# The 18 emptiest experts two by two in one block, with float32 products on two halves of the columns

## The chip, the core and the metric

The kernel runs on one core of a Trainium2 chip. The metric is device time in microseconds (us) of one launch. Of the engines, PE (TensorE) multiplies matrices, DVE (VectorE) and ACT (ScalarE) work elementwise, POOL (GpSimd) issues the indexed transfers here, and SP (SyncE) issues the others. The profile is of one execution.

## The reference

A decoder block: two token mixers side by side (HGRN2 and gated DeltaNet), merged and added to the input, then a mixture of experts, then a final norm. There are 1024 tokens of width 1024 behind 16 learned meta tokens that are dropped at the end. Cut to the part that the change touches:

```python
grp = argmax(g_logits)                         # 4 groups of 8 experts
top_p, top_i = top_k(softmax(e_logits[grp]), 2)
weights = p_grp * top_p / sum(top_p)           # two experts per token
for each expert e, over its tokens x:
    y = (silu(x @ w_gate[e]) * (x @ w_up[e])) @ w_down[e]   # 1024 -> 512 -> 1024
    out[token] += weight * y
return rmsnorm(h + out)
```

There are 32 experts, each with 6 MiB of float32 weights. How many tokens an expert has is known on the chip alone. With the inputs of these runs the fullest of the first 29 experts has 137 tokens, the next ten 65 or more, and the other 18 have 36 to 63; experts 29, 30 and 31 have 60, 53 and 56.

## The kernel before

The mixers fill the first 1000 us or so. What follows is a loop over experts, one step each, in the order 31, 30, 29, 0 to 28. A table made on the chip (`tabi`, `rowi`, `wsl`) says for each expert which rows of the normed stream fill its block of `CB = 112` rows, where the result goes, and with what weight. `pick` finds the fullest of experts 0 to 28 and trades its place with expert 12 (`PQ`); that step works on two blocks (a column `NE` of the table holds the second). Any further rows over 112 would go to a loop at the end that runs only if there are some (`overflow` makes its table; here it has none).

A step works like this. Six transfers of 1 MiB each (`fetch`, issued by SP: gate 2, up 2, down 2) bring the weights into a ring of 12 buffers (`raws`); towards the end the ring shrinks to four, one buffer every 16 transfers from the sixtieth on, because the buffers are wanted for the output. `wload` splits each half of such a buffer in a high and a low part in float32r: ACT copies the high part (line 60) and DVE subtracts it from the source (line 61). When both halves are split, the buffer is free for the next transfer. Rows of tokens are gathered by POOL (line 1233), transposed (line 1244) and split in the same way. `stage_gu` makes three products for each piece, high by high, low by high and high by low (lines 1261 to 1263): 48 products of 512 columns for gate and up. `stage_h` transposes the activation (line 1279) and `stage2` makes 24 more products for down (lines 1299 to 1301). ACT scales the result, and POOL adds it to the residual stream in DRAM by an indexed transfer with accumulation, the scatter (line 1310): 112 rows of 4 KB, whether a row holds a token or a spare row.

The down products of a step stand behind the gate and up products of the next one in TensorE's program, since they wait for the activation (`pend`). The last expert is not scattered; its result is added to the output tiles by products with a one-hot matrix (line 1417), and the final norm follows (from line 1378 on).

Of the kernel before, what the change touches and what calls it, by code (L numbers as in the profile page):

```python
# [19 lines left out]
P = 128  # L20
# [12 lines left out]
def block_kernel(ctx, tc, x, meta_tokens, hg_lb_logits, norm_mix_g, w_in, gd_conv_w, gd_A_log, gd_dt_bias,  # L33
# [191 lines left out]
    NE, NX, CB = 32, 20, 112  # L225
    PQ = 12
    ND = NE - 3
    NT = SEQ // CB
    NB = NE + NX
# [9 lines left out]
    ionb = iota("ionb", NB)  # L239
# [815 lines left out]
    S0, S1 = slice(0, ND), slice(NE, NB)  # L1055
    tabbed = rows(ptb[:, ND:NE], slice(ND, NE))
    tab1 = r_("tab1", [P, NE])
    V.tensor_copy(tab1, ptb[:, 0:NE])
    pei = r_("pei", [1, NE], I32)
    ohx = r_("ohx", [P, NE])  # L1060
    nohx = r_("nohx", [P, NE])
    pxx = r_("pxx", [P, NE])
    ptx = r_("ptx", [P, 1])

    def pick(after):

        with tc.issue_after(after.ins):
            cnt = off[:, NC:NC + 1, 0:ND]
            V.memset(ohx, 0.0)
            first_max("px", cnt, ND, ohx[:, None, 0:ND])  # L1070
            V.tensor_scalar(nohx, ohx, -1.0, 1.0, op0=ALU.mult, op1=ALU.add)
            V.tensor_copy(pxx, ionb[:, 0:NE])
            trade(pxx)
            V.tensor_copy(pei, pxx[0:1])
            trade(tab1)
            return rows(tab1[:, S0], S0)

    def trade(t):
        m = r_next([P, NE])
        V.tensor_tensor(m, t, ohx, op=ALU.mult)  # L1080
        V.tensor_reduce(out=ptx, in_=m, op=ALU.add, axis=AX.X)
        V.tensor_tensor(m, t, nohx, op=ALU.mult)
        V.scalar_tensor_tensor(t, ohx, t[:, PQ:PQ + 1], m, op0=ALU.mult, op1=ALU.add)
        V.tensor_copy(t[:, PQ:PQ + 1], ptx)

    def r_next(shape):
        return rp.tile(shape, F32, name="ptm", tag="ptm")
# [3 lines left out]
    def weigh(after):  # L1091

        with tc.issue_after(after.ins):
# [13 lines left out]
            V.tensor_copy(wsl[:, 0:NE], pw[:, 0:NE])  # L1107
            V.tensor_tensor(wsl[:, 0:NE], wsl[:, 0:NE], pw[:, NE:], op=ALU.add)
            trade(wsl[:, 0:NE])
# [4 lines left out]
    def overflow():  # L1114

        gtx = r_("gtx", [P, NE, NT])
# [3 lines left out]
        zne = r_("zne", [P, NE])  # L1120
# [46 lines left out]
        V.scalar_tensor_tensor(xe, xo, pxx[0:1, PQ:PQ + 1], xe, op0=ALU.mult, op1=ALU.add)  # L1167
# [9 lines left out]
    XB, RMIN, DROP = 2, 4, 16  # L1177
# [8 lines left out]
    for pool, tag, n, b in ((mix, "xl", 4, 1), (rawp, "tg", 1, 1), (rawp, "oh", 2, 1), (wp, "wr", 0, 2), (tl, "bo", 2, 2),  # L1186
                            (mix, "xh0", 2, 1)):
        if n == 0:
            raws.append([pool.tile([P, 1024], F32, name=f"rawh{i}", tag=tag, bufs=b) for i in range(2)])
        else:  # L1190
            t_ = pool.tile([P, n, 2048], F32, name="raw" + tag, tag=tag, bufs=b)
            raws += [[t_[:, i, 0:1024], t_[:, i, 1024:], t_[:, i]] for i in range(n)]
# [5 lines left out]
    sg, hh0 = (wp.tile([P, 512], F32, name="msg" + str(i), tag="st", bufs=3) for i in range(2))  # L1198
    hT = mo.tile([P, 2, 4, CB], F32R, name="hT")
    turn = {"h": 0, "l": 0, "x": 0, "y": 0}  # L1200
# [7 lines left out]
    def fetch(load, src, q):  # L1208
        if nraw[0] > 60 and nraw[0] % DROP == 0 and len(ring) > RMIN:
            ring.pop(0)  # L1210
        wr = raws[ring[0]]
        ring.append(ring.pop(0))
        nraw[0] += 1
        if len(wr) == 2:
            for a in range(2):
                load(wr[a], src, q * 2048 + a * 1024, 1024)
        else:
            load(wr[2], src, q * 2048, 2048)
        return wr

    def wload(load, src, q):
        wr = early.pop(0) if early else fetch(load, src, q)
        nuse[0] += 1
# [8 lines left out]
    def gather(xg, gidx):  # L1232
        nc.gpsimd.indirect_dma_start(out=xg[:CB], out_offset=None, in_=hf_dr,
                                     in_offset=bass.IndirectOffsetOnAxis(ap=gidx[:CB], axis=0),
                                     bounds_check=SEQ, oob_is_err=False)
# [37 lines left out]
    def stage_h(hhs):  # L1273
        r = []
        for i, hh in enumerate(hhs):
# [4 lines left out]
            if i:  # L1280
                hx = rp.tile([P, 2, 4, CB], F32R, name="hx", tag="ohs1")
                hTh, hTl = hx[:, 0], hx[:, 1]
            else:
                hTh, hTl = hT[:, 0], hT[:, 1]
# [24 lines left out]
    def scatter(yt, ridx):  # L1309
        nc.gpsimd.indirect_dma_start(out=h2_dr, out_offset=bass.IndirectOffsetOnAxis(ap=ridx[:CB], axis=0),  # L1310
                                     in_=yt[:CB], in_offset=None, bounds_check=SEQ + P, oob_is_err=False,
                                     compute_op=ALU.add)
# [14 lines left out]

    order = list(range(NE - 1, ND - 1, -1)) + list(range(ND))
    gq = [(n, e) for n, o in enumerate(order) for e in ([PQ, NE] if o == PQ else [o])]
    got = []  # L1330

    def ahead(m):

        while len(got) < len(gq) and gq[len(got)][0] <= m:
            i, e = len(got), gq[len(got)][1]
# [4 lines left out]
            gather(xg, tabi[:, e:e + 1])  # L1340
            got.append(xg)

    def gathered(n):
        ahead(n)
        return [stage_x(got[i]) for i in range(len(gq)) if gq[i][0] == n]


    for e, srcs in ((0, (wg_e, wu_e)), (1, (wg_e, wu_e)), (0, (wd_e,)), (2, (wg_e, wu_e))):
        early += [(by_expert(order[e]), src, q) for src in srcs for q in range(2)]
    early = [fetch(*a) for a in early[:len(raws)]]  # L1350

# [3 lines left out]
    for n, e in enumerate(order):  # L1355
        load = by_expert(e) if e >= ND else by_index(pei[:, e:e + 1])
        if n == NE - 1:
            stage2(*pend)
# [114 lines left out]
```

## Time and profile before

| | us |
|---|---|
| median of 3 runs | 1655.86 (1651.85 to 1659.97) |
| the profiled execution | 1652.94 |
| its span in the trace | 1651.1 |
| PE busy | 1574.7 (95%) |
| DVE busy | 1081.5 |
| ACT busy | 796.1 |
| POOL busy | 224.1 |

The granted clock of TensorE was 0.981 of its full 2.4 GHz in the mean. The span runs from the first to the last instruction of the core; the profiled execution's own time is 1.8 us longer. The share of time in which an engine is busy says nothing yet of which one sets the pace, because the mixers and the expert loop have different limits. The loop is therefore read by windows of time, and from the waits inside these.

### The profile page before, as it was taken

The numbers are of one execution on the slowest core, as the hardware profiler recorded it, in microseconds if no ns is written. First come the engines' busy times: TensorE is split into PE (matmuls) and PEld (weight loads), VectorE is DVE, ScalarE is ACT, GpSimd is POOL, SyncE is SP. The second block draws the span as 40 slices with busy tenths as digits, with TensorE's granted clock in tenths as the row PEclk, the third lists the DMA queues.
The fourth block names the chain that finished last, engine by engine and source line by source line (L and its number), as shares of the span: only waits on it lengthen the run. The fifth ranks groups of instructions, "written<-read, shape, count | busy, mean of one in ns | idle before, by whom it ended". The sixth has DMA issues, their size and how long they took to land. (4 is left out here: it accounts for less than half of the span.)

```text
span 1651.1 us, 27239 instructions
## 1 busy us (share of the span) xinstructions
PE 1574.7 (95%) x10434; PEld 1301.8 (79%) x10434; DVE 1081.5 (66%) x1774; ACT 796.1 (48%) x1171; POOL 224.1 (14%) x172
## 2 busy tenths in 40 slices
PE   6999999999999999999999986999999999999984
PEld 6989898788788778788797885777777777777762
DVE  7224566368367364232647547999999689998976
ACT  6122222332331432322333233888888678888873
POOL 2150000010010010000001012651111111111112
PEclk9999999999999999999999997999999999999996
DMA  6264344344335235267847665999999999999994
GB/s 207 69 208 137 103 129 121 97 128 138 114 103 159 72 89 139 59 181 251 248 140 231 204 230 175 358 332 375 380 371 385 308 316 375 363 363 363 364 343 191
DMA packets 197894, 368.20 MB, mean 223 GB/s; under 512 B 29980, under 2 KB 136670, under 8 KB 175360
## 3 DMA queue, kind: packets, MB, share of 16 engines
q1 hardware_dynamic: 174464, 320.14, 55.9%
q0 software_dynamic: 8320, 23.08, 6.2%
q10 hardware_dynamic: 14976, 23.21, 4.0%
q8 instruction: 83, 1.36, 0.3%
q14 instruction: 51, 0.42, 0.1%
HBM read 311.05 MB, written 62.07 MB: 226 GB/s over the span
## 5 line engine op out<-in xcount | busy, mean ns | idle before, releaser
L284 PE MATMUL pj<-xh,wh 128*128 128x512 f32 (+2 forms) x832 | 307.6, 370 | 0.0
L286 PE MATMUL pj<-xh,wl 128*128 128x512 f32 (+2 forms) x832 | 306.8, 369 | 0.0
L285 PE MATMUL pj<-xl,wh 128*128 128x512 f32 (+2 forms) x832 | 305.9, 368 | 0.0
L284 PEld LDWEIGHTS pj<-xh,wh 128*128 128x128 f32 x832 | 156.7, 188 | 17.1 <-issue 0.2
L286 PEld LDWEIGHTS pj<-xh,wl 128*128 128x128 f32 x832 | 156.8, 188 | 16.7 <-issue 0.6
L285 PEld LDWEIGHTS pj<-xl,wh 128*128 128x128 f32 x832 | 156.6, 188 | 15.9
L345 ACT ACTIVATE st<-pj 128x512 f32<-128x512 f32 (+2 forms) x104 | 54.8, 527 | 169.7 <-PE pj L286 161.8
L1263 PE MATMUL pgu<-mwl,xTs 128*112 128x512 f32 x318 | 126.0, 396 | 0.0
L61 DVE TENSOR_TENSOR wl<-wr,wh 128x1024 fp32r<-128x1024 f32 x44 | 53.7, 1220 | 83.2 <-ACT wh L60 73.1
L1261 PE MATMUL pgu<-sx,xTs 128*112 128x512 f32 x264 | 107.0, 405 | 0.0
L60 ACT ACTIVATE mwh<-rawxl 128x1024 fp32r<-128x1024 f32 x86 | 90.5, 1059 | 33.3 <-PE pgu L1262 22.0
L1262 PE MATMUL pgu<-sx,xTs 128*112 128x512 f32 x264 | 104.8, 397 | 0.8 <-DVE xTs L61 0.8
L1261 PE MATMUL pgu<-mwh,xTs 128*112 128x512 f32 x264 | 104.2, 395 | 0.0
L1262 PE MATMUL pgu<-mwh,xTs 128*112 128x512 f32 x264 | 103.7, 393 | 0.0
L60 ACT ACTIVATE sx<-rawxl 128x1024 fp32r<-128x1024 f32 x84 | 87.9, 1059 | 30.9 <-PE pgu L1262 14.6
L60 ACT ACTIVATE wh<-wr 128x1024 fp32r<-128x1024 f32 x44 | 46.6, 1058 | 108.1 <-PE pj L285 87.6
L309 POOL TENSOR_TENSOR rn<-ss,mhalf 128x4 f32<-128x4 f32 x16 | 20.6, 1286 | 535.9 <-DVE ss L320 305.7
L1310 POOL DMA_INDIRECT h_dr<-h,rowi x32 | 61.8, 1932 | 218.5 <-ACT h L1305 203.9
L1263 PE MATMUL pgu<-sx,xTs 128*112 128x512 f32 x210 | 83.6, 398 | 0.1
L61 DVE TENSOR_TENSOR mwl<-rawxl,mwh 128x1024 fp32r<-128x1024 f32 x57 | 69.3, 1223 | 13.1 <-ACT mwh L60 10.8
L1023 PE MATMUL pyo<-wo,mm 128*128 128x256 f32 x256 | 73.6, 288 | 3.7 <-ACT mm L1001 3.7
L1024 PE MATMUL pyo<-wo,mm 128*128 128x256 f32 x256 | 72.7, 284 | 0.0
(615 smaller groups left out, 3760.4 us busy)
## 6 DMA issues: line engine op xcount, KB each, us to landing
rawxl<-in_w_up_dram SPq DMA_DIRECT2D x36, 1024.0 KB
rawxl<-in_w_down_dram SPq DMA_DIRECT2D x33, 1024.0 KB
wr<-in_w_in_dram SPq DMA_DIRECT2D x44, 512.0 KB
rawbo<-in_w_down_dram SPq DMA_DIRECT2D x19, 1024.0 KB
rawxl<-in_w_gate_dram SPq DMA_DIRECT2D x16, 1024.0 KB
rawxh<-in_w_gate_dram SPq DMA_DIRECT2D x15, 1024.0 KB
rawbo<-in_w_gate_dram SPq DMA_DIRECT2D x13, 1024.0 KB
rawoh<-in_w_gate_dram SPq DMA_DIRECT2D x10, 1024.0 KB
```

The costliest lines, as they stand in the source:

```text
L60: act(out=hi, in_=src, func=AF.Copy)
L61: return eng.tensor_tensor(out=lo, in0=src, in1=hi.bitcast(F32), op=ALU.subtract)
L284: nc.tensor.matmul(ps[:, :n], wh[:, k], a, start=(k == 0), stop=False)
L285: nc.tensor.matmul(ps[:, :n], wh[:, k], b, start=False, stop=False)
L286: last = nc.tensor.matmul(ps[:, :n], wl[:, k], a, start=False, stop=(k == KD - 1))
L345: act(out=st[:, :n], in_=ps, func=func, scale=scale)
L1023: nc.tensor.matmul(ps[:, 0:256], mm[0][:, k, ts], wo[:, 0, k], start=(k == 0), stop=False)
L1024: nc.tensor.matmul(ps[:, 0:256], mm[0][:, k, ts], wo[:, 1, k], start=False, stop=False)
L1261: nc.tensor.matmul(ps[:CB], xTh[:, kk], wh[:, s], start=(kk == 0), stop=False)
L1262: nc.tensor.matmul(ps[:CB], xTl[:, kk], wh[:, s], start=False, stop=False)
L1263: nc.tensor.matmul(ps[:CB], xTh[:, kk], wl[:, s], start=False, stop=(kk == 7))
L1310: nc.gpsimd.indirect_dma_start(out=h2_dr, out_offset=bass.IndirectOffsetOnAxis(ap=ridx[:CB], axis=0), in_=yt[:CB], in_offset=None, bounds_ ...
```

## The change

The experts 0 to 28 are ranked by their count on the chip. `pick` makes one key per expert (count times 32, plus a number that breaks ties), counts for each how many keys are greater, makes a permutation matrix of these ranks, and by one product the list `pei` of experts in order of rank (line 1085). `ranked` permutes the columns of the row table by a transpose and four products (lines 1099 to 1107). Ranks 0 to 10 are worked on alone, as before, with the split weights and 112 rows (`stage_gu`, `stage2`; rank 0 has the second block, column `NBB`). Ranks 11 to 28 form nine pairs: rank 11 + p with rank 20 + p share one block of 128 rows, 64 (`CL`) each.

A pair's weights are not split. Its products take the float32 weights from the ring buffers as they come (`raw`), the token tile is not split either (`pair_x`), and the products of the two experts stand alternately on the first and the last 64 columns of the array (`pair_mm`): 16 and 16 for gate and up and 8 and 8 for down, each of 512 columns. The result is scattered in two transfers of 64 rows (`rowi`, `rowb`), one for each expert, since a token may be in both.

The order becomes experts 31, 30, 29, then pairs and single experts in turn, a pair last. The ring has 11 buffers (the two halves of the twelfth became the pair's token tiles), and it shrinks only within the last 12 transfers. `overflow` shifts the positions of the paired experts, whose block ends at 64 rows, so that rows over 64 would go to the extra blocks, of which there may now be 24.

```diff
+    CL = P // 2
     ND = NE - 3
+    NF = 11
+    NPR = (ND - NF) // 2
...
     def pick(after):
         with tc.issue_after(after.ins):
-            cnt = off[:, NC:NC + 1, 0:ND]
-            first_max("px", cnt, ND, ohx[:, None, 0:ND])
...
-            trade(pxx)
-            trade(tab1)
-            return rows(tab1[:, S0], S0)
+            V.tensor_tensor(ktmp, key, ident[:, 0:NE], op=ALU.mult)
+            V.tensor_reduce(out=kcol, in_=ktmp, op=ALU.add, axis=AX.X)
+            V.tensor_scalar(ktmp, key, kcol, None, op0=ALU.is_gt)
+            V.tensor_reduce(out=rank, in_=ktmp, op=ALU.add, axis=AX.X)
+            V.tensor_scalar(perm, io128[0:NE, 0:NE], rank[0:NE], None, op0=ALU.is_equal)
+            ps = pr("prk2")
+            nc.tensor.matmul(ps[0:1, 0:NE], pid[0:NE], perm, start=True, stop=True, skip_group_check=True)
+            V.tensor_copy(pei, ps[0:1, 0:NE])
...
+            t = ranked(tab1)
+            rows(t[:, 0:NW], slice(0, NW))
...
     def fetch(load, src, q):
-        if nraw[0] > 60 and nraw[0] % DROP == 0 and len(ring) > RMIN:
+        if nraw[0] >= NFETCH - 12 and nraw[0] % 3 == 0 and len(ring) > RMIN:
             ring.pop(0)
...
+    def pair_mm(ps, lhsT, ws, s, start, stop):
+        for hs, w in zip(HALVES, ws):
+            nc.tensor.matmul(ps[hs], lhsT[:, hs], w[2][:, s], start=start, stop=stop, skip_group_check=True)
+
+    def pair_gu(xT, loads):
+        pgu = []
+        for src in (wg_e, wu_e):
+            ps = psp.tile([P, 512], F32, name="pgu", tag="pj")
+            for q in range(2):
+                ws = [raw(load, src, q) for load in loads]
+                for k in range(4):
+                    kk = q * 4 + k
+                    pair_mm(ps, xT[:, kk], ws, slice(k * 512, (k + 1) * 512), kk == 0, kk == 7)
+            pgu.append(ps)
+        act(out=sg, in_=pgu[0], func=AF.Silu)
+        V.tensor_tensor(hh0, sg, pgu[1], op=ALU.mult)
+        return hh0
...
+    def pair_down(cols, loads, hx):
+        py = [pr("pyd") for _ in range(2)]
+        for q in range(2):
+            ws = [raw(load, wd_e, q) for load in loads]
+            for k in range(2):
+                kk = q * 2 + k
+                for g in range(2):
+                    pair_mm(py[g], hx[:, kk], ws, slice(k * 1024 + g * 512, k * 1024 + (g + 1) * 512), kk == 0, kk == 3)
...
+    def scatter(yt, ridx, n=CB):
+        for r, ix in [(slice(0, n), ridx)] if n == CB else zip(HALVES, ridx):
...
-    order = list(range(NE - 1, ND - 1, -1)) + list(range(ND))
+    steps = [(c,) for c in range(NBB - 1, NW - 1, -1)]
+    full = [(c, NBB) if c == 0 else (c,) for c in range(NF)]
+    full = full[2:8] + full[0:2] + full[8:]
+    for c in range(NPR):
+        a, b = (NF * c // (NPR - 1) for c in (c, c + 1))
+        steps += [(NF + c,)] + full[a:b]
```

The programs show what moves. First TensorE at the first step behind the three fixed experts; `phh` is the activation's transpose, `pgu` gate and up, `pyd` down, `pxg` the transpose of gathered rows. Before:

```order
L1300 MATMUL pyd_10317<-mwh1_9897,hT_9904 112x512
L1301 MATMUL pyd_10317<-sx_9895,hT_9904 112x512
L1279 MATMUL phh_10357<-ident_69,msg1_9903 128x112 x4
L1261 MATMUL pgu_10374<-sx_9895,xTs_9901 112x512
L1262 MATMUL pgu_10374<-sx_9895,xTs_9901 112x512
L1263 MATMUL pgu_10374<-mwl0_9898,xTs_9901 112x512
```

And now:

```order
L1335 MATMUL pyd_10325<-mwh1_9900,hT_9910 112x512
L1336 MATMUL pyd_10325<-sx_9898,hT_9910 112x512
L1314 MATMUL phh_10365<-ident_69,msg1_9908 128x112 x4
L1362 MATMUL pgu_10392<-rawoh_9895,xTp0_9905 64x512 x8
L1362 MATMUL pgu_10392<-rawbo_9896,xTp0_9905 64x512 x8
L1362 MATMUL pgu_10413<-rawxh0_9897,xTp0_9905 64x512 x8
L1362 MATMUL pgu_10413<-rawxl_9893,xTp0_9905 64x512 x8
L1279 MATMUL pxg_10439<-ident_69,h40_9887 128x112 x4
```

The products of a pair read the ring buffers themselves (`rawoh` and so on) and fill 64 rows of the result each. A row with x8 is eight products, four for each half in turn.

Then TensorE at the first expert, where the ranking's products stand (`prk2` the list of experts, `prt` the permuted table). Before:

```order
L1244 MATMUL pxg_9928<-ident_69,h40_9882 128x112 x4
L1261 MATMUL pgu_9935<-sx_9895,xTs_9901 112x512
L1244 MATMUL pxg_10032<-ident_69,h41_9883 128x112
L1262 MATMUL pgu_9935<-sx_9895,xTs_9901 112x512
L1263 MATMUL pgu_9935<-sx_9895,xTs_9901 112x512
```

And now, behind all 48 products of that expert:

```order
L1298 MATMUL pgu_9972<-mwl0_9901,xTs_9904 112x512
L1085 MATMUL prk2_10014<-perm_9874,pid_1026 1x32
L1099 MATMUL prt_10021<-ident_69,tab1_9869 32x128
L1279 MATMUL pxg_10037<-ident_69,h41_9888 128x112 x4
L1279 MATMUL pxg_10044<-ident_69,h41_9888 128x112 x4
L1296 MATMUL pgu_10107<-sx_9898,xTs_9904 112x512
L1314 MATMUL phh_10051<-ident_69,msg1_9908 128x112 x4
L1103 MATMUL prt_10021<-perm_9874,tT_10023 128x11
L1105 MATMUL prt_10021<-perm_9874,tT_10023 64x9 x2
L1107 MATMUL prt_10021<-perm_9874,tT_10023 64x9
L1297 MATMUL pgu_10107<-sx_9898,xTs_9904 112x512
```

Seven small products of the ranking are new, and the transposes of the second expert's rows stand behind the first expert's products instead of between them.

Last POOL's gathers and scatters, with what each waits for besides its own order (`DMASW` is the landing of an indexed transfer). Before:

```order
L1310 DMA h_dr<-h_9885,rowi 1153x1024 [waits DMASW1_49,Activation_49]
L1233 DMA xg_10830<-hf_dr,tabi 112x1024 [waits DMASW2_49,PE_49]
L1310 DMA h_dr<-h_9884,rowi 1153x1024 [waits DMASW4_49,Activation_49]
L1233 DMA h_9882<-hf_dr,tabi 112x1024 [waits DMASW0_49,PE_49]
```

And now, around the first pair:

```order
L1404 DMA h_dr<-h_9890,rowi 1153x1024 [waits DMASW1_49,DVE_49,Activation_49]
L1404 DMA h_dr<-h_9890,rowb 1153x1024 [waits DMASW4_49]
L1268 DMA xg_10802<-hf_dr,tabi 112x1024 [waits DMASW2_49,PE_49]
L1404 DMA h_dr<-h_9889,rowi 1153x1024 [waits DMASW5_49,Activation_49]
L1268 DMA h_9887<-hf_dr,tabi 128x1024 [waits DMASW0_49,PE_49]
```

A pair's second scatter waits for the landing of the first, and the next gather stands behind both.

## Rows read from the trace of the kernel before

**Rows 1.** Page: PE busy time, bytes in 40 slices of 41.3 us

```profile
PE 1574.7 (95%) x10434; PEld 1301.8 (79%) x10434; DVE 1081.5 (66%) x1774; ACT 796.1 (48%) x1171; POOL 224.1 (14%) x172
...
GB/s 207 69 208 137 103 129 121 97 128 138 114 103 159 72 89 139 59 181 251 248 140 231 204 230 175 358 332 375 380 371 385 308 316 375 363 363 363 364 343 191
```

**Rows 2.** Windows of the expert loop: us, five engines busy (x instructions), PEclk, DMA share, GB/s

```profile
1020.00:1060.00 40.00, 39.02 (x193) 30.40 (x192) 39.60 (x75) 30.65 (x36) 13.75 (x9) 1.00 0.92 321
1060.00:1280.00 220.00, 220.00 (x1038) 170.68 (x1037) 206.16 (x219) 185.87 (x220) 61.51 (x39) 1.00 1.02 370
1280.00:1340.00 60.00, 60.00 (x277) 46.26 (x276) 40.96 (x41) 39.25 (x49) 7.85 (x5) 1.00 0.91 306
1340.00:1540.00 200.00, 200.00 (x932) 154.31 (x931) 183.22 (x178) 169.41 (x200) 33.43 (x23) 1.00 1.01 363
1540.00:1612.00 72.00, 67.03 (x304) 50.08 (x303) 59.26 (x58) 53.95 (x66) 6.12 (x4) 0.99 0.98 346
```

**Rows 3.** Waits in 1030:1600: us in total, times, longest

```profile
PE pyd L1299 <- ACT hT L60: 1.3, 1, 1.3
...
SPq L1323 <- DVE mwl L61: 238.3, 100, 5.4
SPq L1323 <- DVE sx L61: 173.8, 73, 5.7
```

**Rows 4.** Timeline of PE, one block: start, us, engine, line, operation

```profile
1199.90 0.39 PE L1261 MATMUL pgu<-mwh,xTs 128*112 128x512 f32 x1
...
1201.29 1.04 PE L1244 MATMUL pxg<-ident,h 112*128 112x112 f32 x8
```

**Rows 5.** Timeline of PE, float32 products of 256 columns (16 records are 8 products)

```profile
215.33 3.82 PE L448 MATMUL pkk<-kq 128*128 128x256 f32 x16
218.80 0.51 PE L286 MATMUL pj<-xh,wl 128*128 128x348 f32 x1
```

**Rows 6.** Timeline of PE, float32 products on groups of 32 columns (64 records are 32)

```profile
158.43 0.76 PE L622 MATMUL hps<-hq,hk 128*32 128x32 f32 x64
159.13 0.43 PE L284 MATMUL pj<-xh,wh 128*128 128x348 f32 x1
```

**Rows 7.** DMA queues in 1020:1612: packets, MB, share of 16 engines

```profile
DMA packets 36212, 210.09 MB, mean 355 GB/s; under 512 B 5605, under 2 KB 5605, under 8 KB 15577
...
q1 hardware_dynamic: 28232, 187.16, 82.2%
q0 software_dynamic: 7936, 22.39, 16.9%
```

**Rows 8.** Queue of the scatters in 1570:1588 (one landed) and 1588:1606 (two)

```profile
q0 software_dynamic: 128, 0.46, 12.8%
...
q0 software_dynamic: 255, 0.92, 28.2%
```

**Rows 9.** Timeline of POOL, two scatters one behind the other

```profile
1092.13 2.26 POOL L1310 DMA_INDIRECT h_dr<-h,rowi  x1 [7.30 <-PE pgu L1262]
...
1103.67 1.71 POOL L1310 DMA_INDIRECT h_dr<-h,rowi  x1 [1.99 <-DMA h_dr<-h,rowi]
```

**Rows 10.** Page: the costliest VectorE operation of the loop (busy, mean ns)

```profile
L61 DVE TENSOR_TENSOR mwl<-rawxl,mwh 128x1024 fp32r<-128x1024 f32 x57 | 69.3, 1223 | 13.1 <-ACT mwh L60 10.8
```

**Rows 11.** Windows ahead of the loop where the clock falls (columns as Rows 2)

```profile
873.00:877.00 4.00, 2.97 (x19) 2.22 (x18) 3.14 (x10) 1.33 (x2) 0.00 (x0) 1.00 0.64 206
877.00:880.00 3.00, 2.40 (x6) 1.94 (x7) 2.79 (x9) 1.06 (x1) 0.00 (x0) 0.52 0.68 229
880.00:884.00 4.00, 4.00 (x18) 3.22 (x17) 2.60 (x7) 0.35 (x1) 0.00 (x0) 0.94 0.97 292
```

**Rows 12.** Timeline of ACT and PE at the last expert

```profile
1610.14 2.00 ACT L60 ACTIVATE mwh<-rawbo 128x1024 fp32r<-128x1024 f32 x2 [1.15 <-DMA rawbo<-in_w_down_dram]
...
1617.09 0.39 PE L1301 MATMUL pyd<-mwl,hT 128*112 128x512 f32 x1
1617.58 0.49 PE L1417 MATMUL pfin<-sx 112*128 112x512 f32 x1
```

More of the change, by code (lines that the diff above doesn't have):

```diff
@@ L1054, in block_kernel @@
     wtf, posf = f2(wts), f2(pos)
-    S0, S1 = slice(0, ND), slice(NE, NB)
-    tabbed = rows(ptb[:, ND:NE], slice(ND, NE))
+    S1 = slice(NBB, NB)
+    tabbed = rows(ptb[:, ND:NE], slice(NW, NBB))
     tab1 = r_("tab1", [P, NE])
@@ L1078, in trade @@
[L1078 to L1087, printed above, removed]
+            V.tensor_scalar(key[:, ND:], keys[:, ND:], float(-NE), None, op0=ALU.add)
@@ new lines, in pick, with ranked @@
+            return V.scalar_tensor_tensor(rowb, ktmp[0:CL, 0:NPR], spare[0:CL], t[0:CL, NW:], op0=ALU.mult, op1=ALU.add)
+    def ranked(t):
+        ps = pr("prt")
+        nc.tensor.transpose(out=ps[0:NE, 0:P], in_=t, identity=ident)
+        tT = rp.tile([NE, P], F32, name="tT", tag="sel")
+        V.tensor_copy(tT, ps[0:NE, 0:P])
+        o = ps[:, 256:256 + NW + NPR]
+        nc.tensor.matmul(o[:, 0:NF], tT, perm[:, 0:NF], start=True, stop=True, skip_group_check=True)
+        for b in range(2):
+            nc.tensor.matmul(o[b * CL:(b + 1) * CL, NF:NW], tT[:, 0:CL], perm[:, NF + b * NPR:NF + (b + 1) * NPR],
+                             start=True, stop=True, skip_group_check=True)
+        nc.tensor.matmul(o[0:CL, NW:], tT[:, 0:CL], perm[:, NF + NPR:ND], start=True, stop=True, skip_group_check=True)
+        return o
@@ L1213, in fetch, with raw @@
         nraw[0] += 1
[L1214 to L1218, printed above, removed]
-        return wr
+        load(wr[2], src, q * 2048, 2048)
+        return wr
+    def raw(load, src, q):
+        nuse[0] += 1
+        return early.pop(0) if early else fetch(load, src, q)
     def wload(load, src, q):
-        wr = early.pop(0) if early else fetch(load, src, q)
-        nuse[0] += 1
+        wr = raw(load, src, q)
         r = []
@@ L1307, in stage2, with pair_x @@
         return pys
[L1309 to L1312, printed above, removed]
+    HALVES = slice(0, CL), slice(CL, P)
+    def pair_x(xg):
+        xT = xTp[next_("p", 2)]
+        xgv = xg.rearrange("t (p k) -> t k p", k=KD)
+        for g in range(2):
+            ps = pr("pxg")
+            for k in range(4):
+                nc.tensor.transpose(out=ps[:, k * P:(k + 1) * P], in_=xgv[:, g * 4 + k], identity=ident)
+            if g:
+                V.tensor_copy(xT[:, 4:8], c3(ps))
+            else:
+                act(out=xT[:, 0:4], in_=c3(ps), func=AF.Copy)
+        return xT
@@ L1354, in block_kernel @@
     first = xT[0][2]
[L1355 to L1358, printed above, removed]
+    for n in range(len(steps)):
+        load = weights(n)
+        if n == len(steps) - 1:
+            down(*pend)
             pend = None
-        hh = stage_gu(xT, load)
+        hh = (pair_gu if paired(n) else stage_gu)(xT, load)
         if n == 0:
             picked = pick(first)
-        if n + 1 < len(order):
+        if n + 1 < len(steps):
             xT = gathered(n + 1)
@@ L1366, in block_kernel @@
         if pend is not None:
[L1367 to L1369 removed]
+            down(*pend)
+        cols_ = [(rowi[:, c:c + 1], wsl[:, c:c + 1]) for c in steps[n]]
+        if paired(n):
+            c = steps[n][0]
+            cols_ = [((rowi[:, c:c + 1], rowb[:, c - NF:c - NF + 1]), wsl[:, c:c + 1])]
+        pend = (n, cols_, load, (pair_h if paired(n) else stage_h)(hh))
         if n == 0:
```

145 lines of the change are left out of this document (98 added, 47 removed).

## Prediction

> **What bounds the kernel now.** I read the page first, for where the time is: PE is busy 95% of the span, and in the last two fifths the bytes run at 308 to 385 GB/s [rows 1]. Both could bound the loop over experts, so I took windows of it next. From 1060 to 1280 PE is busy all 220 us, and the DMA engines show a share of 1.02, which I take as their full value; the window from 1340 to 1540 reads 1.00 and 1.01 [rows 2]. Then the waits. PE's products wait for a split once, for 1.3 us, while SP's transfers wait for the splits of the weights, that is, for a buffer to come free, over 400 us in all [rows 3]. So from 1020 to 1612 PE sets the pace (a buffer comes free only as fast as products are made), and the loads stand only just behind it: 40 x 0.92 + 220 x 1.02 + 60 x 0.91 + 200 x 1.01 + 72 x 0.98 = 588 us of a full stream in 592 us. A change that takes work from PE alone would find the stream of loads right behind it. The question is what the stream gains.
>
> **PE's work.** 220 us hold 1038 instructions, and a block has 48 + 24 products and 12 transposes, 84 in all; so a block takes 84 / 1038 x 220 = 17.8 us, and 33 blocks 587 us. The change leaves 15 such blocks (11 ranked, one second block, 3 fixed): 267 us. A pair adds 24 float32 products on each half. Eight float32 products of 256 columns begin at 215.33 and the next product at 218.80 [rows 5]: 0.434 us each, so 0.868 us for 512 columns; a product of the split kind takes (1201.29 - 1199.90) / 6 = 0.232 us [rows 4]. The trace of before has no product on half of the columns with 512 to move. Its nearest row has groups of 32 columns: 32 products in 159.13 - 158.43 = 0.70 us, 22 ns each, where 32 / 256 of 0.434 us would be 54 ns each one after another [rows 6]. So products on different column groups run side by side there, 2.4 at a time over four groups. For two groups I take two at a time, 24 x 0.868 = 20.8 us for a pair; the other end is 41.7 us, as if one after another. Eight transposes of 112 columns take 1.04 us [rows 4], so twelve of 128 take 1.8. A pair is then 22.6 us, nine are 203 us, and PE has 470 us of work for a stream of some 570. It is no longer the bound, by 100 us, and stays clear of the stream until a pair takes (570 - 267) / 9 = 33 us.
>
> **The stream of loads.** The weights stay the same 192 MiB, and so do their transfers; an indexed transfer of weights for a pair costs SP one register load more per pair, which lies beside transfers of 2.7 us each. What goes is scatter. Before, 32 blocks were scattered with 112 rows, 3584 in all (the last is not); after, 15 x 112 + 8 x 128 = 2704, 880 fewer. Their queue moves its 22.39 MB in 16.9% of the engines' time, against 187.16 MB in 82.2% for the weights [rows 7], so a byte there costs 1.7 times as much. One scatter of 112 rows takes 12.8% of 18 us = 2.30 us, two 28.2% of 18 us = 5.08 us [rows 8], 20.6 to 22.7 ns for a row. So 880 rows are 18.1 us, with 20.0 as the upper end; the lower end is nothing, if the stream is held by bytes rather than by its engines' time. Gathers get fewer rows to land only where a slot is empty, and those move nothing; I take nothing.
>
> Next, holes. From 1280 to 1340 the share is 0.91 (the step with two blocks: 35.6 us of PE for six transfers), from 1540 to 1612 it is 0.98 (the shrunken ring): (1.02 - 0.91) x 60 + (1.02 - 0.98) x 72 = 9.5 us of the stream's time that a slower PE left empty [rows 2]. With PE 100 us ahead, and the ring whole until the last 12 transfers, they are filled: -9.5, lower end nothing. One buffer fewer is loaded ahead of the loop: 1.05 MB at 187.16 MB / (0.822 x 592 us) = 385 GB/s is +2.7.
>
> Then the end. Before, the last weights landed at 1610.14 and the first product of the tail began at 1617.58, 7.4 us, with a split and the last products between [rows 12]. After, no split stands there: a transfer is followed by four pairs of products, 3.5 us (6.9 at half the clock). I take -2.0, the range being -3.9 to nothing.
>
> **What I cost at nothing.** The ranking: ten VectorE operations on tiles of 32 columns; the costliest one of the loop, on 1024 columns, takes 1.22 us [rows 10], so they are under 12 us, beside the first expert's 48 x 0.232 = 11.1 us of products, and the table's seven products stand behind these. Without that cover it is 5 us at most, once. The second scatter of a pair waits for the first to land, and POOL's next gather stands behind it. In the trace a scatter that was waited for (one began at 1092.13, the next at 1103.67 [rows 9]) held POOL by some 11.5 us, with other work in between; a step is 18 us or longer, and the gather's rows are needed a step later, so PE still has them. If not, nine pairs would add up to 11.5 us each to PE, 104 us against its 100 us to spare: 4 us. The operations added to `overflow` run once, beside products, on a VectorE that splits for 15 steps instead of 32.
>
> **The sum**, against the profiled execution of 1652.94: -18.1 - 9.5 + 2.7 - 2.0 = -26.9, 1626.0. The median of the runs is 2.9 above that execution, so I forecast 1629. Its own range is 1612 to 1645: with half of the scatter and of the holes and nothing at the end it is 1656 - 14 + 3 = 1645; with all upper ends (20.0, 9.5, 0, 3.9) it is 1622, and 1612 with a third of what rival D would add.
>
> The stream ran at 370 GB/s for 220 us [rows 2]. The Trainium skill, DMA: Bandwidth & Descriptors, section Specifications, gives an HBM bandwidth of some 358 GB/s per core. By that figure the bytes after, 210.09 MB less 880 rows of 4 KB and with the one buffer more, would take 207.5 / 358 = 580 us, and the time would be near 1642 by an estimate. The trace ran above this figure for 220 us, so the measurement decides.
>
> **Rivals.** *A, the halves don't overlap with 512 columns to move.* For it: no row shows that shape. Against: rows 6. A pair would be 41.7 + 1.8 = 43.5, PE 267 + 9 x 43.5 = 659 us against 587, +72: 1728, slower. It decides above 36 us for a pair, where PE is back at 592 us. Chance 0.10.
> *B, the clock falls in the pairs.* A pair needs 12 transfers of 2.7 us, 33 us, and PE works 23 us of these, in pieces with a wait before each. The granted clock fell to 0.52, the level of 1.2 GHz, from 877 to 880, behind a stretch in which PE was busy 2.97 of 4 us, and was back at 0.94 from 880 to 884 [rows 11]. With 1.2 GHz throughout, a pair is 41.7 + 3.6 = 45.3 us, PE 675, +88: 1744, slower. Against it: at that clock PE is busy without a pause, and it was in such a stretch that the clock came back. The Trainium skill, TensorE: Matmul & The Clock Gate, section HAM oscillation, describes bursts that each end in a wait for loads and get the lower clock again and again; nothing in the loop of before shows that, since PE never waited in it. Chance 0.06.
> *C, fewer scattered rows don't speed the loads.* The engines' time that a scatter takes may be latency in which the weights' packets go on. For it: the bytes saved are 3.6 MB of 210, 1.7%. Against: the share is full at 1.02, with both queues in it. Then -9.5 + 2.7 - 2.0 = -8.8, 1647. Chance 0.12.
> *D, the loads go faster without PE behind them.* The best slice of the page had 385 GB/s [rows 1]: 207.5 MB are 539 us against 592, so -53 - 2: 1601. For it: SP then keeps more transfers open at a time. Against: the share is full in the long windows. Chance 0.12.
> *E, an expert of rank 11 or later has more than 64 tokens,* and the extra blocks at the end run with their own loads. The fullest of these has 63; chance 0.02, slower.
>
> **How the numbers follow.** The forecast has 0.58, A 0.10, B 0.06, C 0.12, D 0.12, E 0.02. Half a per cent, 8 us, is about what a measurement can tell from no change; it lies at 1648 and 1664. Faster: the forecast, D and a bit under half of C, 0.75; slower: A, B and E, 0.17 less a little for partial ones, which go to the same, plus the rest of C: 0.08. The range leaves A, B and E outside (0.18) and reaches from D (1601, with 3 below) to a partial A, 1662, in which a pair takes 38 us.
>
> **What would show it.** In the profile after: PE busy near 80% in the loop and waiting for transfers of weights in the pairs; consecutive products of a pair 0.43 us apart (0.87 would be A); DMA share full from 1020 to the end; the scatters' queue below 16.9%; SP hardly waiting for buffers in the pairs; a granted clock at 1.00 in the pairs (0.5 would be B). The forecast is wrong if the loop from 1020 to the last load takes over 580 us, or if PE waits for gathered rows.

## The result, and the profile after

The changed kernel takes 1599.64 us (median of 4 runs, 1598.64 to 1603.7) against 1657.49 us before (4 runs). The ratio is 0.966, with a 95% interval from 0.9629 to 0.9692: faster by 58 us (51 to 61 by the interval), where the forecast had 27. It is outside the forecast's own range (1612 to 1645) and inside the whole range only because that reached to rival D: the time is that of D (1601), not that of the forecast (1629).

The page of the kernel after, PE's busy time and the bytes of its 40 slices (40 us each), to be set against [rows 1]:

```profile
PE 1496.9 (94%) x9915; PEld 1135.5 (71%) x9915; DVE 803.3 (50%) x1516; ACT 541.1 (34%) x884; POOL 191.0 (12%) x162
...
GB/s 209 72 192 145 97 137 137 90 124 169 62 108 148 108 82 118 110 80 254 248 181 185 203 177 211 259 348 360 386 390 388 399 391 391 403 366 400 402 374 212
```

TensorE is busy 94% of the span, where it was 95%. Of the eleven slices ahead of the last, nine reach 386 to 403 GB/s, the other two 366 and 374; before, eight of these eleven have 363 to 385, the others 308, 316 and 343. By windows of the loop (us, five engines' busy time, granted clock, DMA share, GB/s), against [rows 2]:

```profile
1020.00:1060.00 40.00, 39.81 (x207) 31.20 (x207) 35.13 (x66) 26.87 (x32) 4.88 (x4) 1.00 0.91 318
1060.00:1280.00 220.00, 206.40 (x884) 110.80 (x884) 102.39 (x138) 87.14 (x111) 48.10 (x40) 0.96 1.00 383
1280.00:1340.00 60.00, 52.28 (x224) 25.75 (x222) 20.49 (x22) 18.72 (x25) 9.65 (x7) 1.00 1.02 390
1340.00:1540.00 200.00, 188.91 (x822) 111.26 (x820) 94.29 (x94) 88.37 (x110) 25.55 (x17) 0.99 1.02 391
1540.00:1560.00 20.00, 18.46 (x82) 7.01 (x80) 0.69 (x1) 1.49 (x3) 1.47 (x1) 1.00 1.00 374
```

The reader is to compare two columns. DMA share in the two long windows (from 1060 and from 1340): 1.00 and 1.02 here, 1.02 and 1.01 before, so both kernels keep the DMA engines full there. GB/s: 383 and 391 here, 370 and 363 before. A full share hid a stream that could be faster. VectorE's column falls from 206 of 220 us to 102.

The queues from 1020 us to the moment at which SP, with all loads of weights issued, issues the first load of the tail (packets, MB, share of 16 engines), before, in 586.4 us:

```profile
q1 hardware_dynamic: 27828, 185.38, 82.1%
q0 software_dynamic: 7936, 22.39, 17.1%
```

And after, in 531.4 us:

```profile
q1 hardware_dynamic: 25246, 183.31, 84.8%
q0 software_dynamic: 6032, 18.78, 15.1%
```

Each share times its window gives DMA engines' time. The scatters and gathers took 100.3 us and take 80.2: -20.0. The weights took 481.4 and take 450.6: -30.8, in two parts. A megabyte took 481.4 / 185.38 = 2.60 us and takes 2.46: -25.4 for 183 MB. And 2.07 MB fewer go in the window: -5.4. Empty time was 0.8% of 586 and is 0.1% of 531: -4.2. From the window's end to the end of the span it was 44.7 us and is 47.2: +2.5. The sum is -52.5, as the spans differ (1651.1 - 1598.6).

The -5.4 and the +2.5 belong together. By the sizes of all packets from 1020 to the end, less the 8.91 MB of the tail's own transfers, 185.46 MB of weights were left at 1020 before and 185.81 are left after: 0.35 MB more, not fewer, +0.9. The window after only ends with more transfers still under way. So the rest, 2.5 - 5.4 - 0.9 = -3.8, is the end's. From the last weights' landing to the first product of the tail it was 1617.58 - 1610.14 = 7.4 us [rows 12]; after, it is 1566.12 - 1562.54 = 3.6 (timeline):

```profile
1562.54 3.65 PE L1362 MATMUL pyd<-rawxh,msg 128*64 128x512 f32 x12 [0.63 <-DMA rawxh<-in_w_down_dram]
1566.12 0.50 PE L1536 MATMUL pfin<-sx 128*128 128x512 f32 x1
```

That with one buffer fewer loaded ahead (1.05 MB) only 0.35 MB more are left is due to a better start of the loop. Before, TensorE waited for the second expert's rows, in the middle of the first expert's products (timeline, before):

```profile
1008.22 0.43 PE L1244 MATMUL pxg<-ident,h 112*128 112x112 f32 x1 [4.05 <-DMA h<-hf_dr,tabi]
```

After, those transposes stand behind the 48 products, and the wait is gone. The window from 1003 to 1020, before and then after:

```profile
1003.00:1020.00 17.00, 12.95 (x45) 9.21 (x44) 10.18 (x29) 7.63 (x9) 0.99 (x1) 0.69 0.50 159
```

```profile
1003.00:1020.00 17.00, 14.89 (x59) 10.85 (x60) 11.34 (x20) 9.28 (x11) 1.22 (x2) 0.79 0.78 266
```

The share rises from 0.50 to 0.78 in these 17 us. Not all of that is gain: in the changed kernel's trace the loop began 3 us later (POOL issued the first gather at 999.64, before at 996.67). What is left of it at 1020 is 1.05 - 0.35 = 0.70 MB, 1.8 us of the stream.

### The profile page after: what moved, and what is told of

Its sections match the earlier page's. It is cut to its first block, busy times and chain, and to the rows that moved or that the text cites. A ratio compares the mean times of both kernels' runs of the same rounds, so it can differ in the third digit from the quotient of the medians.

```text
span 1598.6 us, 25206 instructions
## 1 busy us (share of the span) xinstructions
PE 1496.9 (94%) x9915; PEld 1135.5 (71%) x9915; DVE 803.3 (50%) x1516; ACT 541.1 (34%) x884; POOL 191.0 (12%) x162
## 5 line engine op out<-in xcount | busy, mean ns | idle before, releaser
L1027 PE MATMUL pyo<-wo,mm 128*128 128x256 f32 x256 | 73.9, 289 | 3.6 <-ACT mm L1005 3.6
L1028 PE MATMUL pyo<-wo,mm 128*128 128x256 f32 x256 | 73.0, 285 | 0.0
L1029 PE MATMUL pyo<-wo,mm 128*128 128x256 f32 x256 | 72.8, 286 | 0.0
L1362 PE MATMUL pgu<-rawxl,xTp 128*64 128x512 f32 x208 | 67.0, 609 | 4.3 <-DMA rawxl<-in_w_up_dram 4.3
L1375 DVE TENSOR_TENSOR msg<-msg,pgu 128x512 f32<-128x512 f32 x9 | 6.2, 688 | 119.3 <-PE pgu L1362 110.9
L1298 PE MATMUL pgu<-mwl,xTs 128*112 128x512 f32 x144 | 57.6, 401 | 2.3 <-DVE mwl L61 2.2
L1404 POOL DMA_INDIRECT h_dr<-h,rowi x23 | 37.8, 1643 | 168.6 <-ACT h L1340 87.7
L1027 PEld LDWEIGHTS pyo<-wo,mm 128*128 128x128 f32 x256 | 49.2, 192 | 4.1 <-ACT mm L1005 4.1
L1001 PE MATMUL pup<-oh,uwl 128*128 128x512 f32 x128 | 51.4, 403 | 0.7 <-DVE uwl L61 0.7
L999 PE MATMUL pup<-oh,uwh 128*128 128x512 f32 x128 | 51.9, 405 | 0.0
L1296 PE MATMUL pgu<-sx,xTs 128*112 128x512 f32 x120 | 49.5, 413 | 1.9 <-ACT sx L60 1.7
L1000 PE MATMUL pup<-ol,uwh 128*128 128x512 f32 x128 | 51.2, 400 | 0.0
## 6 DMA issues: line engine op xcount, KB each, us to landing
rawbo<-in_w_down_dram SPq DMA_DIRECT2D x12, 1024.0 KB, 10.8
```

The source lines that it names most:

```text
L999: nc.tensor.matmul(ps, wh[:, kk], oh[:, kk], start=(k == 0), stop=False)
L1001: nc.tensor.matmul(ps, wl[:, kk], oh[:, kk], start=False, stop=(k == 3))
L1027: nc.tensor.matmul(ps[:, 0:256], mm[0][:, k, ts], wo[:, 0, k], start=(k == 0), stop=False)
L1028: nc.tensor.matmul(ps[:, 0:256], mm[0][:, k, ts], wo[:, 1, k], start=False, stop=False)
L1029: nc.tensor.matmul(ps[:, 0:256], mm[1][:, k, ts], wo[:, 0, k], start=False, stop=(k == 7))
L1298: nc.tensor.matmul(ps[:CB], xTh[:, kk], wl[:, s], start=False, stop=(kk == 7))
```

## The experiments

All kernels were timed beside the kernel before in several rounds. The times are medians; each kernel's ratio to before is given with its interval, and is taken to the kernel before in the same rounds (medians of 1654.96 to 1656.07 in those of this section).

**Is TensorE or the stream what held the kernel before?** One of the three products left out, with all loads, splits and scatters kept:

```diff
-                        nc.tensor.matmul(ps[:CB], xTl[:, kk], wh[:, s], start=False, stop=False)
...
-                        nc.tensor.matmul(py[g], hTl[:, kk], wh[:, s], start=False, stop=False)
```

> The kernel before with the middle product of each three left out (low by high, 24 of 72 products of a block; the result lacks that part). The loads, the splits, the 12 buffers and the 3584 scattered rows stay. TensorE's work in the loop falls from 587 to some 391 us. Theory 1 (before, TensorE alone held the loop, and a full DMA share hid that the stream could go faster): the time falls to what the stream needs with these rows, the 540 us that it took after the change plus 880 rows x 21.6 ns = 19, 559 us against 592: about 1625, the weight transfers' 8 KB packets get shorter. Theory 2 (the stream was itself at its limit, 588 us, and what made it faster after the change was fewer rows, no splits in the pairs and whole 8 KB packets): 4 to 6 us less at most, about 1652, packets as before (mean 338 ns).

Measured: 1645.87, ratio 0.9947 (0.9928 to 0.9965). Neither theory's number. TensorE's waits in this kernel, from 1020 to 1600 (us, times, longest), name a third engine, VectorE with its splits, and the kernel's window from 1060 to 1280 shows VectorE busy 201 of 220 us:

```profile
PE pgu L1262 <- DVE mwl L61: 25.8, 49, 1.7
PE pgu L1262 <- DVE sx L61: 21.1, 38, 1.2
```

```profile
1060.00:1280.00 220.00, 185.88 (x743) 117.49 (x742) 201.42 (x233) 174.21 (x213) 120.68 (x43) 0.95 1.00 363
```

**Without VectorE's splits.** The low parts of the weights left out, the subtraction and the product that reads it:

```diff
-                split(wh, wl, wr[g])
+                act(out=wh, in_=wr[g], func=AF.Copy)
...
-                        nc.tensor.matmul(ps[:CB], xTh[:, kk], wl[:, s], start=False, stop=(kk == 7))
```

> The kernel before without the low parts of the weights: VectorE's subtraction and the product that reads it are left out (the product of the low part of the tokens stays), so two products of three, ACT's copies, the same loads, ring and scatters. Against the kernel with two products and the subtraction (1645.9, VectorE busy 92% and waited for by TensorE) this takes VectorE's 24 x 1.22 us per three steps away. If VectorE was the next bound behind TensorE: 1615 to 1630. If the loads themselves were at their limit of some 360 GB/s: 1643 to 1647.

Measured: 1626.02, 0.9823 (0.9799 to 0.9846), in the range of "VectorE was next". With TensorE and VectorE both relieved, the same loads, ring and 3584 scattered rows run at 374 GB/s in the window from 1060 to 1280, where [rows 2] have 370 and the kernel with two products 363:

```profile
1060.00:1280.00 220.00, 172.98 (x732) 120.84 (x731) 29.03 (x48) 171.00 (x210) 28.89 (x24) 0.94 1.02 374
```

So before the change three limits stood close behind each other: TensorE, 9 us further VectorE's splits, and 20 us or so further the stream. (The prediction had two, TensorE and the stream. ACT's copies, busy 171 of 220 us, are close too; but the last kernel of this section keeps them, gathers fewer rows and is 36 us faster, so it was not they that held this one.)

**Put the splits back into the changed kernel.** The pairs' weights are split too, though nobody reads the result:

```diff
...
+        if too:
+            for g in range(2):
+                split(whs[next_("h", len(whs))], wls[next_("l", len(wls))], wr[g])
...
```

> The changed kernel, in which ACT and VectorE also split the weights of the pairs, as they did before the change; nobody reads the result. A buffer is then released by the splits as well as by the products. If the splits' traffic in the on-chip memory or their pace was what held the loads of before at 355 to 363 GB/s, the rate falls back to that: 206 MB / 0.36 = 572 us against 540, about 1630, and the mean 8 KB packet goes from 321 back to some 337 ns. If the splits don't touch the loads: 1600 to 1603.

Measured: 1628.22, 0.9832 (0.9804 to 0.9861): +28.6, half of the whole gain. But not in the way that was expected of longer packets. Its queues from 1020 to its last issue, 554.9 us:

```profile
q1 hardware_dynamic: 25165, 182.71, 81.6%
q0 software_dynamic: 6032, 18.78, 14.8%
```

A megabyte of weights takes 0.816 x 554.9 / 182.71 = 2.48 us, as in the changed kernel; the share of both together is 96.4%, so 20 us are empty. More than half of that is one place, where `overflow` builds its table. The window from 1095 to 1125 with the splits, and then without:

```profile
1095.00:1125.00 30.00, 20.11 (x79) 10.48 (x79) 19.45 (x31) 13.79 (x15) 20.67 (x18) 0.72 0.55 206
```

```profile
1095.00:1125.00 30.00, 25.28 (x106) 11.56 (x108) 8.22 (x18) 4.49 (x7) 13.30 (x18) 0.83 0.91 342
```

POOL's sixteen operations for that table, with the splits, and then without:

```profile
1086.85 24.19 POOL L1189 TENSOR_SCALAR oht<-io,slot 128x128 fp32r<-128x128 f32 x16 [0.53 <-DVE xst L1170]
```

```profile
1088.05 15.67 POOL L1189 TENSOR_SCALAR oht<-io,slot 128x128 fp32r<-128x128 f32 x16 [2.66 <-DVE xst L1170]
```

24.2 us against 15.7, for the same operations: POOL is slower beside a busy VectorE. (The median operation takes 0.60 us in both; the longest 7.30 and 3.16.) TensorE's products on the table stand in its order and wait there 5.6 us for POOL and 3.9 for VectorE with the splits, 2.1 and 2.7 without; the loads wait for the buffers that TensorE still needs. The share of 0.55 instead of 0.91 in 30 us is 10.8 of the 28.6 us.

The slow operations alone don't make the hole. In the kernel before they took as long, beside a VectorE that was splitting:

```profile
1051.02 24.07 POOL L1151 TENSOR_SCALAR oht<-io,slot 128x128 fp32r<-128x128 f32 x16 [3.39 <-DVE slot L1143]
```

But there they were done at 1075, and TensorE came to its products on the table at 1080 and didn't wait. After the change the chain starts at 1087 to 1088, behind what was added to `overflow`.

**Put the scattered rows back.** A third scatter behind each pair, of 110 spare rows:

```diff
+        if n != CB:
+            nc.gpsimd.indirect_dma_start(out=h2_dr, out_offset=bass.IndirectOffsetOnAxis(ap=sparei[0:110], axis=0), ...
```

> The changed kernel with a third scatter behind each pair that adds 110 rows to spare rows, so that 8 x 110 = 880 rows are scattered again, as many as before the change. If a scattered row costs the stream 21.6 ns, as the forecast has it: +19, 1619. If rows cost the stream nothing, as the 16 us saved by skipping empty slots brought only 2: 1600 to 1603. A third way: POOL's longer chain of three scatters makes gathers late, then TensorE waits for gathered rows in the profile.

Measured: 1616.95, 0.977 (0.9741 to 0.98): +17.3, 19.7 ns a row. Its queues in 552.3 us, 98.3 us for the indexed queue against 80.2:

```profile
q1 hardware_dynamic: 25445, 184.79, 82.4%
q0 software_dynamic: 7440, 22.39, 17.8%
```

**Take empty rows out.** Empty slots get a row number out of bounds, in the kernel before and in the changed one:

```diff
-        return V.scalar_tensor_tensor(rowi[:, s], emp[:, s], spare, ps, op0=ALU.mult, op1=ALU.add)
+        return V.scalar_tensor_tensor(rowi[:, s], emp[:, s], BIG, ps, op0=ALU.mult, op1=ALU.add)
```

> The kernel before, with empty slots of a block given a row number out of bounds, so that the scatter skips them: about 2000 rows instead of 3584, 1580 x 21.6 ns = 34 us less work for the DMA engines, TensorE's work unchanged at 587 us. Theory 1: no change beyond 5 us, since TensorE holds the loop (1651 to 1657). Theory 2: the stream becomes free by 34 us and TensorE is next at once, so also no more than 5 us; but a DMA share of some 0.94 instead of 1.0, where theory 1 leaves open that packets get longer or shorter.

> The changed kernel with empty slots skipped by the scatter: about 1950 rows instead of 2704. If the scattered rows cost the stream 21.6 ns each, as the forecast has it, 750 rows are -16 us: 1583 to 1585. If rows cost the stream nothing (rival C of the forecast): 1597 to 1601. If shorter queues of scatters also shorten the weights' packets, more than -16: 1575.

Measured: before, 1656.73, 1.0007 (0.9995 to 1.0019), no change, as both theories had it. Its queues from 1020 to 1612, against [rows 7], show where the time of the rows went:

```profile
q1 hardware_dynamic: 28297, 187.24, 84.8%
q0 software_dynamic: 7936, 15.85, 11.5%
```

The indexed queue gives back 5.4% of 592 us, 32 us. About half of it is empty time now. The other half has gone into the weights, which take 2.68 us per megabyte instead of 2.60: while TensorE holds the loop, the same packets get longer (mean 349 ns, where the kernel before has 337). So the time per megabyte is not a fixed price of the stream, and a nearly full share doesn't show that the stream is the limit.

After, 1597.97, 0.9663 (0.9641 to 0.9685), the same as the changed kernel within the intervals, where 1584 was expected; no kernel here that does all the work beats the changed one beyond the intervals. The rows did go (the changed kernel with skipping, 526.9 us; 64.8 us for the indexed queue):

```profile
q1 hardware_dynamic: 25086, 182.24, 85.7%
q0 software_dynamic: 6032, 15.72, 12.3%
```

What was saved came back as empty time: 98.0% of 526.9 us are filled, 10.5 us are not. Its windows from 1060 to 1280 and from 1340 to 1540 show 382 GB/s at a share of 0.99 where the changed kernel had 383 and 391 at 1.00 and 1.02:

```profile
1060.00:1280.00 220.00, 205.16 (x885) 109.83 (x881) 100.73 (x137) 84.05 (x106) 48.66 (x41) 0.97 0.99 382
1340.00:1540.00 200.00, 188.53 (x825) 111.59 (x826) 94.33 (x94) 88.08 (x109) 26.86 (x18) 0.99 0.99 382
```

So a row costs some 20 ns while the stream is the limit, and beyond the changed kernel's 2704 rows taking more away gains nothing. Which limit is then next was not tried; TensorE is busy 205 of 220 and 189 of 200 us there, and from 1060 to 1540 SP waits 118 us for products of the pairs that still read a buffer, more than for VectorE (56).

**Both put back together.**

> The changed kernel with both put back: the pairs' weights are also split by ACT and VectorE (alone +28.6: 1628.2), and 880 more rows are scattered (alone +17.3: 1617.0). If the two costs add (each is paid where the other leaves no room): 1599.6 + 46 = 1645, and some 10 us of the gain over 1655.9 are TensorE's. If the splits leave holes in the stream that the rows can fill (20 us of holes in the first, 18 us of rows in the second): 1628 to 1632.

Measured: 1648.18 (1639.79 to 1651.03), 0.9954 (0.9939 to 0.997): the costs add, +48.5 against 28.6 + 17.3 = 45.9. Of the gain of 58 us, some 8 are left for all the rest. Its weights still take 2.47 us per megabyte, in packets of 319 ns: the shorter packets by themselves are worth little.

**The halves in another order.** A pair's products four by four instead of one by one:

```diff
-                for k in range(4):
-                    kk = q * 4 + k
-                    pair_mm(ps, xT[:, kk], ws, slice(k * 512, (k + 1) * 512), kk == 0, kk == 7)
+                for h in range(2):
+                    for k in range(4):
+                        kk = q * 4 + k
+                        half_mm(h, ps, xT[:, kk], ws, slice(k * 512, (k + 1) * 512), kk == 0, kk == 7)
```

> The changed kernel with a pair's products in another order: four (down: also four) of the first half of the columns, then four of the second, instead of one by one in turn. If two products run side by side only where they stand next to each other, only one seam of eight overlaps: 24 x 2 x 0.868 x 7/8 = 36.5 us for a pair's products instead of 20.8, TensorE's work 267 + 9 x 38.3 = 612 us, and the loop is held by TensorE again: about 1655 + 20 = 1675. If the order makes no difference: 1600.

Measured: 1608.41, 0.9726 (0.9705 to 0.9746): +9, neither number. The timeline (start, us) has records of the two halves, from two buffers, still 60 ns apart:

```profile
1242.19 0.59 PE L1362 MATMUL pgu<-rawxl,xTp 128*64 128x512 f32 x1
1242.25 0.59 PE L1362 MATMUL pgu<-rawtg,xTp 128*64 128x512 f32 x1
1242.62 0.59 PE L1362 MATMUL pgu<-rawxl,xTp 128*64 128x512 f32 x1
1242.68 0.59 PE L1362 MATMUL pgu<-rawtg,xTp 128*64 128x512 f32 x1
```

The second half's products start while up to four records of the first are still to come. Standing next to each other in the program is not needed for running side by side here. A pair's 64 records of gate and up, where nothing interrupts them, take 16.06 us (from 1060.3 on) instead of 13.95 in turn (from 1061.4 on); that the beginning and end of each chain lose these 2 us fits the timeline, but wasn't tried.

**Why do the weights take less time per megabyte?** Four kernels changed one difference each: 7 buffers instead of 11 (`ring = list(range(7))`); all transfers issued as two halves; and, on the kernel without the low parts, 11 whole buffers without the twelfth in halves, and gathers of 8 rows for a block instead of 112. (That one leaves most rows out: the products are made all the same, on what the buffer held.)

> The changed kernel with 7 buffers in the ring instead of 11, so that some 5 transfers are outstanding as in the second half of the kernel before, not 9 to 10. If the number of outstanding transfers sets the rate of the stream: back to 360 GB/s, about 1630. If it only covers the alternation of pairs and single experts, 7 buffers hold 19 us of the stream, a little more than half of a pair's 12, and TensorE would wait more in pairs and the loads in single steps: 1605 to 1615.

> The changed kernel with each transfer of weights issued as two halves, so that all packets have 4 KB, as every twelfth buffer had before the change. By the packets' means of the kernel before (177 ns for 4 KB, 338 for 8 KB) a byte takes 5% longer: +24 us, 1624; by their medians (159 and 309 ns) 3%: +14, 1614. The twelfth of before would then be worth 1 to 2 us. If the stream is held by bytes and not by its engines' time: 1600 to 1603.

> The kernel before without the low parts of the weights (1626.0), and with the ring of 11 whole buffers that the changed kernel has, so that no transfer is issued in halves of 4 KB packets. If the halves of one buffer in twelve make the packets of 8 KB longer too (mean 333 to 337 ns in all kernels that have them, 319 to 321 where no halves are): the mean falls to some 321 ns and the time by 15 to 20, about 1608. If the halves cost only their own packets: 1622 to 1626, packets as they were.

> The same kernel without the low parts (1626.0, ring of 12 with the halves), gathering 8 rows for a block instead of 112 (the other rows of a block are what was there). Weight packets that overlap a gathered row had a mean of 373 to 407 ns in the kernels with the order of before and 350 to 355 in those of after; beside no indexed packet 324 to 330 and 313 to 315. If the gathers are what lengthens the packets: mean 8 KB packet some 321 ns, and the time 1626 less 12 (the packets) and up to 18 (the rows' own 1900 x 160 ns / 16) = 1596 to 1614. If they are not: packets as before (333 ns), and no more than the rows' own 18: 1608 to 1626.

| kernel | us | ratio (95%) | mean packet of 8 KB, 1060 to 1540 |
|---|---|---|---|
| before | 1657.49 | 1 | 337 ns |
| before, empty rows skipped | 1656.73 | 1.0007 (0.9995 to 1.0019) | 349 |
| two products | 1645.87 | 0.9947 (0.9928 to 0.9965) | 335 |
| no low parts | 1626.02 | 0.9823 (0.9799 to 0.9846) | 333 |
| no low parts, whole buffers | 1624.13 | 0.9818 (0.9778 to 0.9858) | 328 |
| no low parts, 8 rows gathered | 1590.3 | 0.96 (0.957 to 0.963) | 324 |
| after | 1599.64 | 0.966 (0.9629 to 0.9692) | 319 |
| after, splits too | 1628.22 | 0.9832 (0.9804 to 0.9861) | 320 |
| after, 880 rows more | 1616.95 | 0.977 (0.9741 to 0.98) | 319 |
| after, 7 buffers | 1624.73 | 0.9806 (0.978 to 0.9831) | 321 |
| after, empty rows skipped | 1597.97 | 0.9663 (0.9641 to 0.9685) | 321 |
| after, splits and rows | 1648.18 | 0.9954 (0.9939 to 0.997) | 319 |
| after, halves in another order | 1608.41 | 0.9726 (0.9705 to 0.9746) | 321 |
| after, half loads | 1609.26 | 0.9718 (0.9691 to 0.9745) | 166 (4 KB) |

The means are taken over the packets of the traces. The typical packet is the same in all of them: the median is 309 to 311 ns before and after. What differs is the share of long ones: 18% take over 330 ns before, 6% after. In the changed kernel, splits, the number of scattered rows and the number of buffers do not set the packets' length. The halves of one buffer in twelve make 5 ns of it, and 2 us in time, which is within the intervals. All transfers in halves cost 9.6 us, less than the 14 by the medians. The gathered rows make 9 ns, and taking most of them away is worth 36 us in that kernel, more than the 12 to 30 that were expected. But before and after gather the same tokens, in 33 blocks and in 24, so that this explains the difference only in part. Why a weight packet beside gathered rows is shorter after the change stays open.

The ring is another matter: with 7 buffers packets are as short, and the time is 25 us longer. Its windows from 1060 to 1280 and from 1340 to 1540:

```profile
1060.00:1280.00 220.00, 199.88 (x840) 106.16 (x839) 99.97 (x135) 84.01 (x106) 47.51 (x39) 0.97 1.00 380
1340.00:1540.00 200.00, 184.48 (x795) 104.06 (x795) 83.32 (x86) 80.23 (x101) 24.55 (x17) 0.98 0.98 372
```

Fewer buffers are filled ahead of the loop (206.31 MB are left from 1020 on, not 202.48), and the stream has holes (a share of 0.98 from 1340 to 1540, not 1.02).

## Why the prediction was right, and where it was not

**The halves side by side: right.** Two records of a pair start 0.01 us apart, the next two 0.43 to 0.48 later (timeline of the changed kernel; a product is two records):

```profile
1228.80 0.64 PE L1362 MATMUL pgu<-rawxl,xTp 128*64 128x512 f32 x1
1228.81 0.64 PE L1362 MATMUL pgu<-rawxh,xTp 128*64 128x512 f32 x1
1229.28 0.59 PE L1362 MATMUL pgu<-rawxl,xTp 128*64 128x512 f32 x1
1229.29 0.59 PE L1362 MATMUL pgu<-rawxh,xTp 128*64 128x512 f32 x1
...
1239.96 1.12 PE L1362 MATMUL pgu<-rawtg,xTp 128*64 128x512 f32 x1 [2.99 <-DMA rawtg<-in_w_up_dram]
```

So 0.86 us for a product of each half, as forecast, and rival A is out. (The range's far edge, 1662, was said to be a pair of 38 us; by rival A's own sum it is one of 36 to 37.) The last row is the wait for a transfer that the forecast had in the pairs. Less slack was left on TensorE than thought: by the windows above it is busy 506 of 540 us, not 80%. The granted clock was 0.96 to 1.00 in the windows, against rival B; it fell to 0.50 from 1100 to 1109, behind the waits for the table.

**The scattered rows: right.** -18.1 was forecast; the queue's time fell by 20, and 880 rows put back cost 17.3. Rival C is out for this step.

**The holes: right in kind, half the size.** -9.5 forecast, -4.2 measured, since 1.02 was taken as full where the sum of both queues says 0.99.

**The start: missed in part.** The transposes' move stands in the order shown with the change, and the wait in the trace; the 1.8 us of the stream that it freed by 1020 had no term. The +2.7 for the buffer fewer was right, and +0.9 is left of it.

**The end: right in kind, more than forecast.** -2.0 forecast, -3.8 measured, at the far end of what it gave (-3.9).

**The step that failed** is the price of a megabyte of weights and, with it, what was costed at nothing. The prediction read "a full stream" from a share of 1.02 and took 385 GB/s for the weights as given. The share was as full after, at 2.46 us for a megabyte instead of 2.60: 25.4 us. With rows taken out of the kernel before, the same megabyte took 2.68. This is rival D's time, and D had a chance of 0.12; that it was met is in part luck, since D's reason is not what the runs show: the forecast named more transfers kept open, and with 7 buffers the packets were as short. (Fewer buffers do cost 25 us, but by empty time.) And the removal of the splits from 18 experts had no term at all, though [rows 3] name VectorE as what SP waits for in over 400 us and [rows 2] show it busy 206 of 220 us. With the splits left in, the changed kernel takes 1628.2. (That this meets the forecast doesn't make its sum right: that kernel has the short packets too, and loses their gain to holes.) So the shorter packets are worth their 25 us only together with the splits' removal; why they are shorter stays open. The VectorE work added to `overflow`, costed at nothing, was not quite hidden: TensorE waits 2.7 us for it (`ptb` for `ohc`) and 2.1 for POOL behind it, where it waited for neither before, and the share is 0.91 in the 30 us around. With the splits left in, 10.8 us more of the stream are empty there.

**The second scatter of a pair: right.** It waits for the first one's landing (POOL, wait in brackets), 7 to 9 us, and from 1020 on no product waits for gathered rows:

```profile
1209.31 1.80 POOL L1404 DMA_INDIRECT h_dr<-h,rowi  x1 [3.84 <-ACT sx L60]
1218.07 2.39 POOL L1404 DMA_INDIRECT h_dr<-h,rowb  x1 [6.96 <-DMA h_dr<-h,rowi]
...
1229.81 1.05 POOL L1268 DMA_INDIRECT h<-hf_dr,tabi  x1 [0.30 <-issue]
```

The Trainium skill, Perfetto Trace Analysis, section Roofline, says that a single core may draw more from its memory than the share of 358 GB/s that it has beside a busy neighbour, bounded by its 16 DMA engines at some 435. The trace agrees (381 GB/s over 531 us, 391 in a window of 200). Weighed against the rule of 358 it would have raised rival D's chance.

## What to carry to other kernels

A DMA share of 1.0 says that packets are always under way, not that bytes can't go faster; the time per megabyte of each queue, and the engine that frees the buffers, say more. Where a profile shows several engines above 90% in the same stretch, count them all: relieving one moved this kernel by 9 us, two by 29. Before a term is put at nothing because it disappears, put it back in a test; here that was half of the gain.

## What was not expected of the hardware

POOL's sixteen compare operations of 128 x 128 took 24.19 us beside a VectorE that was splitting all weights (24.07 in the kernel before) and 15.67 beside one that split fewer; most took 0.60 us in either, and a few were held up, the longest for 7.30 us. The Trainium skill, Trainium Architecture — The Big Picture, section What this means for kernel authors, has VectorE and GpSimd share a port by an exclusive lock, and the engines' side and the DMA side of the on-chip memory not contend; the first agrees with this, the second with weight packets of 320 ns with the splits and 319 without.

A row that the scatter skips leaves an 8-byte packet of some 10 ns in the trace, where a row that it adds takes 327 ns (median).
